# A two-layer image transformer on one core: the last tile of the merge by halves, two tiles per expert choice, the first gather from a product, the late loop elsewhere

## The chip, the cores and the metric

The kernel runs on one core of one Trainium2 chip. The metric is the device time of one execution in microseconds (us): the median of three runs before the change is 2968.36 us (2964.67 to 2971.39). Three engines matter most here. TensorE (PE; its weight loads are shown as PEld) multiplies matrices and takes its instructions strictly in their order; VectorE (DVE) and ScalarE (ACT) do the element work; GpSimd (POOL) issues the indirect transfers (gathers and scatters by a list of rows), and SyncE (SP) issues the weight loads.

## The reference, cut to what matters

Two layers (DEPTH = 2), each a mixer (retention, windowed and global attention) followed by a mixture of experts. Layer 0 has 6 tiles of 128 tokens (512 image and 256 context tokens), layer 1 only the 4 image tiles. What the change touches is the end of the mixer and the experts:

```python
y, yc = mixer_sublayer(...)            # ends with: y @ w_out
x = x + gt1 * y
h = rms_norm(x, g_norm2[l]) * (1.0 + sc2) + sh2
scores = jax.nn.sigmoid(tokens @ w_router)          # 16 experts in 4 groups
biased = scores + b_router
group_score = lax.top_k(biased by group, 2)[0].sum(-1)
group = jnp.argmax(group_score); local = lax.top_k(in_group, 2)[1]
weight = scores of the two / their sum
hid = jax.nn.silu(xb @ w_gate[e]) * (xb @ w_up[e]);  y = hid @ w_down[e]
out = for each token the weighted sum of its two experts' y
```

Everything is float32; the matrix products of the experts have D = 1024 and a hidden width of 512.

## The kernel before, in words

**Merge.** For each tile of 128 tokens `out_phase` (L1471) multiplies by `w_out` in two halves of 512 columns; `evac_o` (L1462) scales each half (`ot`) and adds it to the tile (`xo`). The generator `second(m)` (L1437) then makes the second norm (`u`, the sum of squares, `rstd`, `h`), stores `h` to `h2d`, transposes it (`h2t`, copied to `h2T`), multiplies by the router weights (`lg`) and goes on into `Router.tile` (L1985), which ranks the experts of one tile on VectorE (`rw`), counts earlier tokens by two small products (`rk`), and has GpSimd scatter a record for each token and choice (`tabd<-recs,ridx`). The table `HOOKS` says at which (half, chunk) of a later tile's product a step of `second` runs; behind the last tile a list of steps runs what is left, with nothing of the product beside it. `R.finish` (L2045) then has ACT read the records of the first three experts back (`rec<-tabd`).

**Experts.** `moe(l)` (L1538) walks 16 slots, each an expert with 12 weight chunks of 512 KB (4 of gate G, up U, down D each), so 192 loads in a layer, issued by SP in the order of use into pools of limited room (class `Weights`). The kinds of the slots are `BBBBPBSBBPBSBPBS` in layer 0 and `BBBSBSSBSSBSSBSS` in layer 1. `B` is a block of 128 tokens, whose weights are split into two words first (`wh` by ACT at L102, `wl` by DVE at L114) and whose product has three terms. `S` (class `Half`) is a block of 64 tokens that is multiplied by the unsplit weights (`raw`). `P` is a pair of both with the same weights: each chunk goes first to the block, then to the half. Each block begins with a gather of its tokens by POOL (L1549, `xg`), a transpose (`xbt`, for a half `xst`) and its evacuation by ACT (`xH`, L182).

**The late loop.** At the start of `moe` (L1771) stands `tc.For_i(0, nmore)`, a loop on all engines over blocks that did not fit their slot. `nmore` is read from memory; with these inputs it is 0, and no instruction of its body runs.

Of the kernel before, what the change touches and what calls it, by code (L numbers as in the profile page):

```python
# [16 lines left out]
D = 1024  # L17
# [9 lines left out]
LB = 2  # L27
# [10 lines left out]
class Weights:  # L38
# [95 lines left out]
    def free_raw(self, c):  # L134
        self.live[id(c.raw_pool)] -= 1
        c.raw_pool = None
        self.load()

# [9 lines left out]
def tile_dit(ctx, tc, a, out):  # L148
# [1181 lines left out]
    def merge(l):  # L1330
# [92 lines left out]
        R = Router(tc, nc, rt, small, l, nm, tri, ones, br, oac_tile, tabd[l])  # L1423
# [12 lines left out]

        def second(m):  # L1437
# [10 lines left out]
            if m == nm - 1:  # L1448
                ws.limit = last_out[l] + NEXT[l]
                ws.load()  # L1450
# [9 lines left out]
            yield from R.tile(m, lo)  # L1460

        def evac_o(m, n, ps):  # L1462
            j = 1 if m >= NIMG else 0
            c = slice(n * 512, (n + 1) * 512)
            t = page("ot1")
            nc.vector.tensor_tensor(t[:, 0:512], ps, gt1[j][:, c], op=OP.mult)
            nc.vector.tensor_tensor(xo[m][:, c], xo[m][:, c], t[:, 0:512], op=OP.add)
            if n == 1:
                load_x(m + 2)

        def out_phase():  # L1471
# [13 lines left out]
            def step(m):  # L1485

                if 0 <= m < nm:
                    if m not in steps:
                        steps[m] = second(m)
                    next(steps[m], None)  # L1490

            chunks = []
            for m in ms:
# [6 lines left out]
                if m == NIMG - 1 and nm > NIMG:  # L1500
                    at[1, 6] = lambda: mod_rows(1)
# [3 lines left out]
                for n in range(2):  # L1505
                    ps = acc_tile(f"pso_{m}{n}")
                    for k in range(8):
# [10 lines left out]
                        if k % 2:  # L1518
                            ws.pump(1)
                            if m == nm - 1:  # L1520
                                ws.free(c)
                    evac_o(m, n, ps)
            ws.set_pools(2 * l, [(raw_p, "raw", RAWB)], [],
                         [(raw_p, "raw", RAWB), (ex, "ex", EX[l]), (pool0, "pg", PG0)], [])
            last = nm - 1
            for b in (0, 1, 0, 1, 0, 2, 0, 1, 0, 0):
                step(last - b)
            for m in ms:
                assert next(steps[m], 0) == 0, m
            R.finish()  # L1530

        drive(branch_gen(), lambda: 2500)
        out_phase()
        st.close()
        return R, late, ex


    def moe(l, R, late, ex):  # L1538
# [5 lines left out]
        ws.set_pools(2 * l + 1, [(raw_p, "raw", RAWB), (pool0, "pg", PG0 - 5 * (l == 0)), (ex, "ex", EX[l])], [(mw, "mw", MW)],  # L1544
# [27 lines left out]
        class Block:  # L1572


            def __init__(self, r, pair=False, slot=None):
                self.r, self.pair, self.slot = r, pair, slot

            def fetch(self, t=None):
                self.t = mx.tile([128, D], F32, tag="xg", name="xg", bufs=XG[l]) if t is None else t
                gather(self.r, self.t)  # L1580
# [50 lines left out]
        class Half(Block):  # L1631
# [4 lines left out]
            def fetch(self):  # L1636
                self.t = mx.tile([128, D], F32, tag="xg", name="xg", bufs=XG[l])
                gather(self.r, self.t, 64)
# [100 lines left out]
        for s in range(NE):  # L1739
            kind = LINES[l][s]  # L1740
            if s < AHEAD:
                blocks.append([Block(R.rec[:, s, :])])
                continue
# [7 lines left out]
        queue = [b for bs in blocks for b in bs]  # L1751
# [19 lines left out]
        with tc.For_i(0, nc.values_load(R.nmore[0:1, 0:1], min_val=0, max_val=SLOTS)) as j:  # L1771
            late_block(j)
# [8 lines left out]
        ahead()  # L1781
        next_record()

        def gate(s, c0, c1, ps, done=None):

            for c in range(c0, c1):
                ch = ws.get()
                for i, b in enumerate(blocks[s]):
                    b.up(ps[i], *words(b, ch), c)
                    if c == 3 and done:  # L1790
                        done(i)
                used(ch)
# [11 lines left out]
        for s in range(NE):  # L1804
# [17 lines left out]
            for k in range(4):  # L1822
                ch = ws.get()
                for b in blocks[s]:
                    b.down(*words(b, ch), k)
                used(ch)
# [3 lines left out]
            for b in blocks[s]:  # L1830
                b.finish()
            if l == 0 and s == NE - 2:
# [45 lines left out]
MORE = 6  # L1878
YO = {0: 2, 1: 1}
# [13 lines left out]
HOOKS = {(0, 0): 1, (0, 1): 2, (0, 4): 1, (0, 5): 3, (1, 0): 2, (1, 3): 1}  # L1893
# [24 lines left out]
class Router:  # L1918
# [3 lines left out]
    def __init__(self, tc, nc, rt, small, l, nt, tri, ones, br, oac_tile, tabd):  # L1922
# [3 lines left out]
        self.rec = small([128, AHEAD, 4], I32, "rec")  # L1926
        self.order = small([128, NS], I32, "order")
# [10 lines left out]
    def prepare(self):  # L1938
# [28 lines left out]
        self.cumf = rt.tile([128, 7, NE], F32, name=f"cumf{l}")  # L1967
        nc.vector.memset(self.cumf[:, 0, :], 0.0)
        nc.vector.memset(self.cum[:, 0, :], 0.0)
        self.idx = rt.tile([128, 6, 2], I32, name=f"ridx{l}")  # L1970
# [14 lines left out]
    def tile(self, m, lo):  # L1985
# [3 lines left out]
        w = rt.tile([128, 16, NE], F32, tag="rw", name=f"rw{l}_{m}", bufs=2)  # L1989
        s = w[:, 0, :]  # L1990
        nc.scalar.activation(s, lo[:, 0:NE], AF.Sigmoid)
        yield
        b = w[:, 1, :]
        tt(b, s, self.br, op=OP.add)
        b4 = b.rearrange("p (g e) -> p g e", e=4)
        t0 = w[:, 2:6, :].rearrange("p a (b c) -> p a b c", b=4)
        t1 = w[:, 6:10, :].rearrange("p a (b c) -> p a b c", b=4)
        rk = w[:, 10, :].rearrange("p (g e) -> p g e", e=4)
        self.ranks(rk, b4, 4, 4, (t0, t1))
        top = w[:, 11, :].rearrange("p (g e) -> p g e", e=4)  # L2000
        stt(top, rk, 2.0, b4, op0=OP.is_lt, op1=OP.mult)
        gs = w[:, 12, 0:4]
        nc.vector.reduce_sum(gs, top, axis=AX.X)
        gr = w[:, 12, 4:8]
        self.ranks(gr[:, None, :], gs[:, None, :], 1, 4, (t0[:, 0:1], t1[:, 0:1]))
        sel = w[:, 12, 8:12]
        nc.vector.tensor_scalar(sel, gr, 0.0, None, op0=OP.is_equal)
        sel16 = sel[:, :, None].to_broadcast([128, 4, 4])
        M = w[:, 13:15, :]
        for j in range(2):  # L2010
            stt(M[:, j, :].rearrange("p (g e) -> p g e", e=4), rk, float(j), sel16, op0=OP.is_equal, op1=OP.mult)
        bb = rt.tile([128, NE], BF16, tag="bb", name=f"bb{l}_{m}", bufs=2)
        tt(bb, M[:, 0, :], M[:, 1, :], op=OP.add)
        tt(self.cumf[:, m + 1, :], self.cumf[:, m, :], bb, op=OP.add)
        nc.vector.tensor_copy(self.cum[:, m + 1, :], self.cumf[:, m + 1, :])

        two = [128, 2, NE]
        tt(w[:, 2:4, :], M, s[:, None, :].to_broadcast(two), op=OP.mult)
        ww = w[:, 15, 0:4]
        nc.vector.reduce_sum(ww[:, 0:2], w[:, 2:4, :], axis=AX.X)  # L2020
        tt(ww[:, 2:3], ww[:, 0:1], ww[:, 1:2], op=OP.add)
        nc.vector.reciprocal(ww[:, 3:4], ww[:, 2:3])
        wd = self.recs[:, m, :, 2:3].bitcast(F32)
        nc.vector.tensor_scalar(wd[:, :, 0], ww[:, 0:2], ww[:, 3:4], None, op0=OP.mult)
# [3 lines left out]
        nc.tensor.matmul(ps[:, 0:NE], self.tri, bb, start=True, stop=False)  # L2028
        nc.tensor.matmul(ps[:, 0:NE], self.ones, self.cum[:, m, :], start=False, stop=True)
        row = w[:, 4, :]  # L2030
        stt(row, ps[:, 0:NE], float(NE), self.eidx, op0=OP.mult, op1=OP.add)
        tt(w[:, 6:8, :], M, row[:, None, :].to_broadcast(two), op=OP.mult)
        nc.vector.reduce_sum(w[:, 15, 4:6], w[:, 6:8, :], axis=AX.X)
        nc.vector.tensor_copy(self.idx[:, m, :], w[:, 15, 4:6])
        for j in range(2):
            nc.gpsimd.memset(self.spacer, 0.0)
            st = nc.gpsimd.indirect_dma_start(
                out=self.tabd, out_offset=bass.IndirectOffsetOnAxis(ap=self.idx[:, m, j:j + 1], axis=0),
                in_=self.recs[:, m, j, :], in_offset=None)
            for o in self.scat:  # L2040
                self.tc.declare_no_dep(st.ins, o.ins, reason="each record has a row of its own")
            self.scat.append(st)
# [194 lines left out]
```

## Time and profile before

| | |
|---|---|
| runs (us) | 2971.39, 2968.36, 2964.67 (median 2968.36) |
| the profiled execution (us) | 2971.79, of which its span 2970.0 |
| mean granted TensorE clock | 0.969 |
| busy: PE, DVE, ACT, POOL | 2774.9 (93%), 1835.0 (62%), 1279.9 (43%), 355.3 (12%) |
| moved by DMA | 557.63 MB, 188 GB/s over the span |
| PE's share of the chain that ended last | 27% by named lines, DMA 6%, DVE 3% |

The span is the time from the first to the last instruction, so what lies around it is 1.8 us. Busy shares are means over stages with different limits: the two expert stages (about 1345 to 1650 us and 2683 to 2946 us of the span) move more than 340 GB/s, the stages before them far less. In the rows a column "[x <-E y]" behind an instruction says how long its engine was idle before it and what ended that.

### The profile page before, as it was taken

The numbers are of one execution on the slowest core, as the hardware profiler recorded it, in microseconds if no ns is written. First come the engines' busy times: TensorE is split into PE (matmuls) and PEld (weight loads), VectorE is DVE, ScalarE is ACT, GpSimd is POOL, SyncE is SP. The second block draws the span as 40 slices with busy tenths as digits, with TensorE's granted clock in tenths as the row PEclk, the third lists the DMA queues.
The fourth block names the chain that finished last, engine by engine and source line by source line (L and its number), as shares of the span: only waits on it lengthen the run. The fifth ranks groups of instructions, "written<-read, shape, count | busy, mean of one in ns | idle before, by whom it ended". The sixth has DMA issues, their size and how long they took to land. (4 is left out here: it accounts for less than half of the span.)

```text
span 2970.0 us, 41952 instructions
## 1 busy us (share of the span) xinstructions
PE 2774.9 (93%) x15152; PEld 2221.7 (75%) x15152; DVE 1835.0 (62%) x3340; ACT 1279.9 (43%) x2370; POOL 355.3 (12%) x415
## 2 busy tenths in 40 slices
PE   7999999999999999979999699999999999978985
PEld 4888888888888766767666378878888887767653
DVE  4676567666554455677676566667776655677543
ACT  4444445445443211217575354444455442226332
POOL 1220000000010000022222131100000100012311
PEclk8999999999999999989999899999999999988998
DMA  6333222213243566758999732222223447589997
GB/s 240 131 110 105 89 75 91 91 65 103 100 156 118 211 240 238 273 225 304 328 370 363 256 122 82 89 78 97 75 96 123 146 153 285 207 304 341 370 367 293
DMA packets 201910, 557.63 MB, mean 188 GB/s; under 512 B 25158, under 2 KB 49862, under 8 KB 201696
## 3 DMA queue, kind: packets, MB, share of 16 engines
q1 hardware_dynamic: 173888, 503.63, 47.0%
q0 software_dynamic: 10688, 25.02, 3.5%
q10 hardware_dynamic: 17120, 26.23, 2.4%
q8 instruction: 121, 1.98, 0.3%
q14 instruction: 93, 0.76, 0.1%
HBM read 461.94 MB, written 96.77 MB: 188 GB/s over the span
## 5 line engine op out<-in xcount | busy, mean ns | idle before, releaser
L114 DVE TENSOR_TENSOR wl<-raw,wh 128x1024 fp32r<-128x1024 f32 x474 | 564.6, 1221 | 130.7 <-ACT wh L102 123.8
L102 ACT CAST wh<-raw 128x1024 fp32r<-128x1024 f32 x474 | 484.4, 1050 | 352.0 <-DMA raw<-oT 105.0
L887 ACT ACTIVATE P<-sc,st 128x768 f32<-128x768 f32 (+4 forms) x240 | 176.3, 734 | 339.9 <-DVE st L885 213.4
L885 DVE TENSOR_REDUCE st<-sc 128x1 f32<-128x768 f32 (+4 forms) x240 | 178.6, 744 | 121.5 <-PE sc L174 115.7
L174 PE MATMUL psb<-wl,wh 128*128 128x512 f32 x480 | 189.6, 395 | 8.1 <-DVE wl L114 8.0
L921 ACT CAST ptH<-pt 128x512 fp32r<-128x512 f32 x264 | 142.9, 591 | 125.0 <-PE pt L906 104.5
L174 PE MATMUL psb<-wh,wh 128*128 128x512 f32 x480 | 192.9, 402 | 1.7 <-ACT wh L102 1.7
L174 PE MATMUL psb<-wh,wl 128*128 128x512 f32 x480 | 189.1, 394 | 2.0 <-DVE wl L114 2.0
L931 DVE TENSOR_TENSOR ptL<-pt,ptH 128x512 fp32r<-128x512 f32 x264 | 169.6, 681 | 9.3 <-ACT ptH L921 9.1
L906 PE MATMUL pt<-ident,P 128*128 128x128 f32 x1056 | 141.5, 275 | 13.9 <-ACT P L887 10.9
L906 PEld LDWEIGHTS pt<-ident,P 128*128 128x128 f32 x1056 | 119.5, 141 | 45.2 <-ACT P L887 31.3
L174 PE MATMUL psR<-wh,hH 128*128 128x512 f32 (+1 forms) x384 | 150.8, 393 | 0.0
L174 PE MATMUL psR<-wl,hH 128*128 128x512 f32 (+1 forms) x384 | 147.1, 383 | 2.7 <-DVE wl L114 2.7
L174 PE MATMUL psR<-wh,hL 128*128 128x512 f32 (+1 forms) x384 | 147.6, 384 | 0.0
L893 DVE TENSOR_SCALAR P<-P,st 128x768 f32<-128x768 f32 (+3 forms) x240 | 130.0, 542 | 8.5
L174 PEld LDWEIGHTS psb<-wh,wh 128*128 128x128 f32 x480 | 91.1, 190 | 47.5 <-issue 19.3
L481 POOL TENSOR_SCALAR rstd<-ss 128x4 f32<-128x4 f32 (+2 forms) x70 | 22.0, 314 | 835.3 <-ACT h L487 303.1
L174 PEld LDWEIGHTS psb<-wl,wh 128*128 128x128 f32 x480 | 91.1, 190 | 29.1 <-DVE wl L114 11.5
L174 PE MATMUL sc<-swkT,swqs 128*128 128x256 f32 x704 | 109.1, 281 | 2.2 <-ACT P L887 2.2
L174 PEld LDWEIGHTS psb<-wh,wl 128*128 128x128 f32 x480 | 91.1, 190 | 22.9 <-DVE wl L114 3.6
L174 PE MATMUL yps<-wh,hidT 128*128 128x512 f32 x320 | 105.7, 397 | 0.0
L1094 DVE COPY sc<-sink 128x1 f32<-128x1 f32 x160 | 25.7, 161 | 128.5 <-PE sc L174 122.3
(495 smaller groups left out, 6916.4 us busy)
## 6 DMA issues: line engine op xcount, KB each, us to landing
raw<-in_w_in_dram SPq DMA_DIRECT2D x136, 512.0 KB
raw<-in_w_gate_dram SPq DMA_DIRECT2D x128, 512.0 KB
raw<-in_w_up_dram SPq DMA_DIRECT2D x128, 512.0 KB
raw<-in_w_down_dram SPq DMA_DIRECT2D x128, 512.0 KB
raw<-in_w_mod_dram SPq DMA_DIRECT2D x96, 512.0 KB
raw<-in_w_br_dram SPq DMA_DIRECT2D x48, 512.0 KB
raw<-oT SPq DMA_DIRECT2D x30, 512.0 KB
raw<-in_w_out_dram SPq DMA_DIRECT2D x16, 512.0 KB
```

The source lines that it names most:

```text
L102: self.nc.scalar.copy(c.h, c.raw)
L114: self.nc.vector.tensor_tensor(c.l, c.raw, c.h.bitcast(F32), op=OP.subtract)
L174: nc.tensor.matmul(ps, lhs, rhs, start=start, stop=stop, skip_group_check=share)
L481: nc.gpsimd.tensor_scalar(r[:, 0:cnt], ss, four / n, four * EPS, op0=OP.mult, op1=OP.add)
L885: nc.vector.reduce_max(st[:, 1, h:h + 1], s[:, 0:self.ns], axis=AX.X, negate=True)
L887: nc.scalar.activation(self.P[h][:, 0:self.ns], s[:, 0:self.ns], AF.Exp, bias=st[:, 1, h:h + 1], accum_out=st[:, 2, h:h + 1])
L893: nc.vector.tensor_scalar(self.P[h][:, 0:self.nk], self.P[h][:, 0:self.nk], st[:, 3, h:h + 1], None, op0=OP.mult)
L906: nc.tensor.transpose(pt[:, c * 256 + h * 128:c * 256 + (h + 1) * 128], self.P[2 * x + h][:, i * 128:(i + 1) * 128], ident)
L921: nc.scalar.copy(ph, src)
L931: nc.vector.tensor_tensor(pl, src, ph.bitcast(F32), op=OP.subtract)
L1094: nc.vector.tensor_copy(s[:, nk:nk + 1], sink[:, hd:hd + 1])
```

## The change

1. The last tile of the merge is worked by halves (class `Last`): squares and `u` of a half as soon as that half is added, its transposes and half of its scores inside the second half's product, and the norm factor applied to the scores (`scores = r * (u @ w_router) + sh2 @ w_router`) rather than to the tokens first; the shift's row is made by nine small products (`shift`).
2. `Router.pair` in place of `Router.tile`: ranks of two tiles in one set of instructions; `HOOKS` gets other places.
3. For the first three experts the row list `first` is made by products of 0/1 matrices (`oh`) with the row numbers (`idc`), and POOL gathers the first block (`x0`) by it before the last pair's scatters. The first three blocks gather by `first`.
4. The late loop stands behind slot 10 in layer 0 and slot 13 in layer 1.
5. In a `P` slot the half's products run behind the block's four chunks (`chunk`), no longer between them.
6. One buffer fewer for late blocks (`LB`), and one page fewer for the weights of layer 1 (x0 holds it).

```diff
-LB = 2
+LB = 1
...
+            def stat(self, n):
+                nc.scalar.activation(self.h[:, c], xo[last][:, c], AF.Square, accum_out=self.ss[:, n:n + 1])
+                nc.vector.tensor_tensor(self.u[:, c], xo[last][:, c], g2[j][:, c], op=OP.mult)
...
+            def end(self):
+                self.norm()
+                self.turn(1)
+                nc.vector.scalar_tensor_tensor(self.h, self.u, self.r[:, 0:1], sh2[j], op0=OP.mult, op1=OP.add)
+                nc.sync.dma_start(h2d[l][last * 128:(last + 1) * 128, :], self.h)
+                nc.sync.dma_start(xa[l][last], xo[last])
+                ws.limit = last_out[l] + NEXT[l]
+                ws.load()
+                self.score(1)
+                s = sg_of(last)
+                nc.vector.scalar_tensor_tensor(s, self.lo[:, 0:NE], self.r[:, 0:1], self.shw, op0=OP.mult, op1=OP.add)
+                nc.scalar.activation(s, s, AF.Sigmoid)
...
+                if m == last:
+                    at[0, 3] = L.begin
+                    at[0, 6] = L.shift
+                    at[1, 6] = lambda: L.turn(0)
...
-            for b in (0, 1, 0, 1, 0, 2, 0, 1, 0, 0):
-                step(last - b)
+            L.end()
+            step(last - 1)
...
+            x0 = pool0.tile([128, D], F32, tag="pg", name=f"x0{l}")
+            for _ in R.pair(last - 1, sg[last // 2], x0):
+                pass
             R.finish()
...
-        with tc.For_i(0, nc.values_load(R.nmore[0:1, 0:1], min_val=0, max_val=SLOTS)) as j:
-            late_block(j)
         ws.limit = first_in + NEAR if l == 0 else len(ws.specs)
         ws.load()
...
+        def chunk(bs, c, step, done=None):
+            ch = ws.get()
+            step(0, c, words(bs[0], ch))
+            if c == 3 and done:
+                done(0)
+            if len(bs) == 1:
+                used(ch)
+                return
+            ws.pump(2, LEAD)
+            ws.free_parts(ch)
+            kept.append(ch)
+            if c == 3:
+                for i, ch in enumerate(kept):
+                    step(1, i, words(bs[1], ch))
+                    ws.free(ch)
...
             for b in blocks[s]:
                 b.finish()
+            if s == LOOPAT[l]:
+                with tc.For_i(0, nc.values_load(R.nmore[0:1, 0:1], min_val=0, max_val=SLOTS)) as j:
+                    late_block(j)
...
+LOOPAT = {0: 10, 1: 13}
-HOOKS = {(0, 0): 1, (0, 1): 2, (0, 4): 1, (0, 5): 3, (1, 0): 2, (1, 3): 1}
+HOOKS = {(0, 0): 1, (0, 4): 1, (0, 5): 2, (1, 1): 1, (1, 5): 1, (1, 7): 1}
...
+    def pair(self, m, s, x0=None):
+        for e in range(AHEAD):
+            oh = rt.tile(shape, BF16, tag="oh", name=f"oh{l}_{m}{e}", bufs=2)
+            tt(oh, self.places[:, None, :].to_broadcast(shape), f[:, :, e:e + 1].to_broadcast(shape), op=OP.is_equal)
+            for i in range(4):
+                nc.tensor.matmul(psf[:, e:e + 1], oh[:, i // 2, :], self.idc[:, i % 2, m + i // 2:m + i // 2 + 1],
+                                 start=i == 0, stop=i == 3)
+            if x0 is not None:
+                tt(self.first[:, e:e + 1], self.firstf[:, e:e + 1], psf[:, e:e + 1], op=OP.add)
+                if e == 0:
+                    nc.gpsimd.indirect_dma_start(
+                        out=x0, out_offset=None, in_=self.h2d,
+                        in_offset=bass.IndirectOffsetOnAxis(ap=self.first[:, 0:1], axis=0))
```

POOL, end of layer 1's merge, before: the last scatters of the records, then the first gather (`xg<-h2d`, by the records that were read back), then the loop.

```order
L2036 MEMSET spacer 1x1
L2037 DMA tabd_122<-recs_23670,ridx_23693 14336x4
L1549 DMA xg<-h2d_119,rec 128x1024
L1771 TENSOR_LOAD nmore
L1771 COMPARE_AND_BRANCH
```

The same place now: L2173 is the gather of `x0` by `first`, L2204 a scatter, L1650 the gather of the second block.

```order
L1531 TENSOR_TENSOR ss<-ss 128x1
L486 TENSOR_SCALAR rstd<-ss 128x1
L487 TENSOR_TENSOR rstd<-rstd,nhalf 128x1
L2173 DMA x_24942<-h2d_119,first 128x1024
L2203 MEMSET spacer 1x1
L2204 DMA tabd_122<-recs_23677,ridx_23705 14336x4
```

The first gather moved ahead of the last pair's four scatters, and the loop left this place.

SP, layer 1, before: the loop's exit (L1771; its body stands ahead of it) is followed by the loads of most of the layer (L83).

```order
L1771 COMPARE_AND_BRANCH
L1771 UNCONDITIONAL_BRANCH
L83 DMA raw_25236<-in_w_up_dram 128x1024
L83 DMA raw_25238<-in_w_up_dram 128x1024
L83 DMA raw_25240<-in_w_up_dram 128x1024
L83 DMA raw_25242<-in_w_up_dram 128x1024
L1776 TENSOR_LOAD order
```

Now the loop (L1949) stands behind the layer's last load; here with the waits printed (`DMAHW0` to `DMAHW7` are the counters of the weight loads):

```order
L83 DMA raw_26987<-in_w_down_dram 128x1024 [waits DMAHW1_49]
L83 ISA
L83 DMA raw_26995<-in_w_down_dram 128x1024 [waits DMAHW2_49,DVE_49]
L1949 TENSOR_LOAD nmore
L1949 ISA x2
L1949 COMPARE_AND_BRANCH
L1949 UNCONDITIONAL_BRANCH [waits SP_sequencer_49,DMAHW0_49,DMAHW1_49,DMAHW2_49,DMAHW3_49,DMAHW4_49,DMAHW5_49,DMAHW6_49,DMAHW7_49]
```

On SP no weight load of layer 1 is left behind the loop, and its exit waits for all eight counters of the loads.

PE, layer 1, the first product of slot 14 (a half; U, then G) before, with the waits:

```order
L1643 MATMUL xst<-ident,xg 128x64 x7
L174 MATMUL u<-raw_27016,xs 64x256 [waits DMAHW1_49]
L174 MATMUL u<-raw_27016,xs 64x256 x3
L174 MATMUL u<-raw_27027,xs 64x256 [waits DMAHW2_49]
L174 MATMUL u<-raw_27027,xs 64x256 x3
```

The same products now, directly behind the loop:

```order
L1745 MATMUL xst<-ident,xg 128x64 x8
L179 MATMUL u<-raw_26834,xs 64x256 x4
L179 MATMUL u<-raw_26840,xs 64x256 x4
L179 MATMUL u<-raw_26847,xs 64x256 x4
L179 MATMUL u<-raw_26851,xs 64x256 x4
L179 MATMUL g<-raw_26855,xs 64x256 [waits Activation_49]
```

The products of the last two slots no longer wait for a load, each of which had its own wait before.

## Rows read from the trace of the kernel before

**Rows 1.** Busy time by stretch: us; PE, PEld, DVE, ACT, POOL; clock; DMA share; GB/s.

```profile
1220.00:1310.00 90.00, 90.00 (x487) 75.11 (x485) 65.77 (x162) 23.72 (x36) 10.36 (x22) 1.00 0.66 248
1310.00:1340.00 30.00, 6.23 (x33) 5.76 (x33) 17.40 (x80) 3.52 (x7) 9.04 (x16) 0.55 0.71 272
1340.00:1350.00 10.00, 7.07 (x19) 5.18 (x20) 5.16 (x5) 6.18 (x6) 3.38 (x3) 0.50 0.34 106
...
1400.00:1650.00 250.00, 250.00 (x1308) 172.14 (x1308) 164.07 (x159) 156.41 (x179) 58.95 (x39) 1.00 0.98 349
2590.00:2650.00 60.00, 60.00 (x312) 49.69 (x311) 43.42 (x92) 16.12 (x23) 4.42 (x10) 1.00 0.82 302
2650.00:2680.00 30.00, 7.51 (x45) 7.03 (x44) 18.49 (x80) 4.03 (x8) 8.12 (x15) 0.57 0.69 255
2680.00:2690.00 10.00, 8.80 (x26) 6.55 (x27) 6.05 (x6) 6.72 (x7) 3.38 (x3) 0.57 0.80 271
...
2700.00:2800.00 100.00, 98.32 (x562) 69.80 (x562) 65.78 (x67) 51.14 (x62) 25.41 (x18) 1.00 1.03 372
...
2918.00:2946.00 28.00, 22.42 (x143) 9.17 (x141) 3.90 (x7) 1.71 (x4) 3.14 (x2) 1.00 0.86 317
```

**Rows 2.** The chain that ended last, end of layer 1: start, us, what.

```profile
2934.19 10.49 DMA raw<-in_w_down_dram
```

**Rows 3.** Timeline of PE, the last two slots of layer 1.

```profile
2918.50 0.71 PE L1643 MATMUL xst<-ident,xg 64*128 64x64 f32 x8
...
2941.85 3.96 PE L174 MATMUL ysm<-raw,hidS 128*64 128x512 f32 x16 [0.52 <-ACT hidS L1674]
```

**Rows 4.** Timeline of VectorE, both merges' ends: start, us, engine line op.

```profile
1308.57 0.69 DVE L1466 TENSOR_TENSOR ot<-pso,m 128x512 f32<-128x512 f32 x1 [0.23 <-PE pso L174]
...
2649.84 0.69 DVE L1466 TENSOR_TENSOR ot<-pso,m 128x512 f32<-128x512 f32 x1 [0.24 <-PE pso L174]
...
2654.86 0.23 DVE L1979 TENSOR_TENSOR rw<-rw 128x64 f32<-128x64 f32 x1
...
2667.57 0.34 DVE L2084 TENSOR_TENSOR sq<-bw 128x169 f32<-128x169 f32 x1
```

**Rows 5.** Timeline of PE in layer 0's experts.

```profile
1344.86 0.79 PE L174 MATMUL g<-wh,xH 128*128 128x512 f32 x1 [1.10 <-ACT xH L182]
...
1546.44 0.39 PE L174 MATMUL yps<-wh,hidT 128*128 128x512 f32 x1
...
1556.71 0.71 PE L1643 MATMUL xst<-ident,xg 64*128 64x64 f32 x8
...
1567.35 0.50 PE L174 MATMUL yps<-wh,hidT 128*128 128x512 f32 x1
...
1572.93 1.03 PE L493 MATMUL xbt<-ident,xg 128*128 128x128 f32 x8
...
1583.41 3.65 PE L174 MATMUL ysm<-raw,hidS 128*64 128x512 f32 x16
```

**Rows 6.** The chain that ended last, end of layer 1's merge.

```profile
2660.44 15.71 DMA tabd<-recs,ridx
2676.15 3.91 issue
...
2683.12 1.22 PE g L174 x2
```

**Rows 7.** Timeline of POOL, then of ACT, end of layer 1's merge.

```profile
2669.04 0.96 POOL L2037 DMA_INDIRECT tabd<-recs,ridx  x1 [0.21 <-issue]
2673.99 0.99 POOL L1549 DMA_INDIRECT xg<-h2d,rec  x1 [3.99 <-SPq L1771]
...
2671.16 0.33 ACTq L2050 DMA_DIRECT2D rec<-tabd  x1
```

**Rows 8.** The loop's line on SP: count, shortest/median/longest ns, first and last start.

```profile
L1771 SPq EVENT_SEMAPHORE  x42: 17/28/28, 1330.0 to 2679.1; - x42
```

**Rows 9.** What SP waited for from 2668 to 2682: us in total, times, longest.

```profile
SPq L1771 <- DMA xg<-h2d,rec: 2.8, 1, 2.8
```

More of the change, by code (lines that the diff above doesn't have):

```diff
@@ L1435, in load_x, with sg_of @@
                 nc.sync.dma_start(xo[m], x_src(m))
+        last = nm - 1
+        sg = {}
+        def sg_of(m):
+            if m // 2 not in sg:
+                sg[m // 2] = rt.tile([128, 2, NE], F32, tag="sg", name=f"sg{l}_{m}", bufs=2)
+            return sg[m // 2][:, m % 2, :]
         def second(m):
@@ L1459, in second, with begin, shift, load_col @@
                 mm(lo[:, 0:NE], hf[:, k * 128:(k + 1) * 128], wr[:, k, :], k == 0, k == 7)
-            yield from R.tile(m, lo)
+            nc.scalar.activation(sg_of(m), lo[:, 0:NE], AF.Sigmoid)
+            yield
+            if m % 2:
+                yield from R.pair(m - 1, sg[m // 2])
+        class Last:
+            def begin(self):
+                self.h = page(f"h2_{l}_{last}")
+                self.u = page(f"u_{l}_{last}")
+                self.hf = page(f"h2T{l}_{last}")
+                self.ss = small([128, 8], F32, "ss", bufs=4)
+            def shift(self):
+                j = 1 if last >= NIMG else 0
+                ps = oac_tile("shr")
+                for k in range(8):
+                    mm(ps[0:1, 0:NE], self.col[:, k:k + 1], wr[:, k, :], k == 0, k == 7)
+                row = rt.tile([1, NE], F32, name=f"shrow{l}")
+                nc.scalar.copy(row, ps[0:1, 0:NE])
+                ps2 = oac_tile("shb")
+                mm(ps2[:, 0:NE], self.one, row, True, True)
+                self.shw = rt.tile([128, NE], F32, name=f"shw{l}")
+                nc.scalar.copy(self.shw, ps2[:, 0:NE])
+            def load_col(self):
+                j = 1 if last >= NIMG else 0
+                self.col = rt.tile([128, 8], F32, name=f"shcol{l}")
+                self.one = rt.tile([1, 128], F32, name=f"onerow{l}")
+                nc.gpsimd.memset(self.one, 1.0)
+                nc.sync.dma_start(self.col, modd[l][j, 3, :].rearrange("(k p) -> p k", p=128))
+            def stat(self, n):
+                j = 1 if last >= NIMG else 0
+                c = slice(n * 512, (n + 1) * 512)
+                nc.scalar.activation(self.h[:, c], xo[last][:, c], AF.Square, accum_out=self.ss[:, n:n + 1])
+                nc.vector.tensor_tensor(self.u[:, c], xo[last][:, c], g2[j][:, c], op=OP.mult)
+            def turn(self, n):
+                ps = oac_tile(f"u2t{l}_{n}")
+                for k in range(4):
+                    c = slice((4 * n + k) * 128, (4 * n + k + 1) * 128)
+                    nc.tensor.transpose(ps[:, k * 128:(k + 1) * 128], self.u[:, c], ident)
+                o = n * 512
+                if n == 0:
+                    nc.scalar.copy(self.hf[:, 0:512], ps)
+                else:
+                    nc.scalar.copy(self.hf[:, o:o + 256], ps[:, 0:256])
+                    nc.vector.tensor_copy(self.hf[:, o + 256:o + 512], ps[:, 256:512])
+            def score(self, n):
+                if n == 0:
+                    self.lo = oac_tile(f"lg{l}_{last}")
+                for k in range(4 * n, 4 * n + 4):
+                    mm(self.lo[:, 0:NE], self.hf[:, k * 128:(k + 1) * 128], wr[:, k, :], k == 0, k == 7)
+            def norm(self):
+                nc.gpsimd.tensor_tensor(self.ss[:, 2:3], self.ss[:, 0:1], self.ss[:, 1:2], op=OP.add)
+                self.r = rstd_of(self.ss[:, 2:3], D, 1)
+            def end(self):
+                j = 1 if last >= NIMG else 0
+                self.norm()
[9 more added lines that the diff above has]
+                nc.scalar.activation(s, s, AF.Sigmoid)
@@ L1750, in moe @@
             blocks.append(bs)
-        queue = [b for bs in blocks for b in bs]
+        queue = [b for bs in blocks[1:] for b in bs]
+        blocks[0][0].t = x0
         later = [b for b in queue if b in records]
@@ L1926, in __init__ @@
         self.rec = small([128, AHEAD, 4], I32, "rec")
+        self.first = small([128, AHEAD], I32, "first")
         self.order = small([128, NS], I32, "order")
@@ L1999, in tile, with by_group @@
[L1999 to L2002, printed above, removed]
+        w = rt.tile([128, 22, 2, NE], F32, tag="rw", name=f"rw{l}_{m}")
+        def by_group(t):
+            return t.rearrange("p j (g e) -> p (j g) e", e=4)
+        b = w[:, 0]
+        tt(b, s, self.br[:, None, :].to_broadcast([128, 2, NE]), op=OP.add)
+        t0, t1 = (w[:, i:i + 4].rearrange("p a j (g e) -> p (a j g e)", e=4).rearrange("p (g a c) -> p g a c", g=8, a=4)
+                  for i in (1, 5))
@@ L2007, in tile @@
+        sel = w[:, 11, 1, 0:8]
         nc.vector.tensor_scalar(sel, gr, 0.0, None, op0=OP.is_equal)
[L2008 to L2024, printed above, removed]
+        sel4 = sel[:, :, None].to_broadcast([128, 8, 4])
@@ L2030, in tile @@
[L2030 to L2034, printed above, removed]
-        for j in range(2):
[L2036 to L2042, printed above, removed]
+        for j in range(2):
+            o = ps[:, j * NE:(j + 1) * NE]
+            nc.tensor.matmul(o, self.tri, bb[:, j, :], start=True, stop=False)
+            nc.tensor.matmul(o, self.ones, self.cum[:, m, :], start=False, stop=j == 0)
+            if j:
+                nc.tensor.matmul(o, self.ones, bb[:, 0, :], start=False, stop=True)
@@ new lines, in pair @@
+        nc.vector.reciprocal(sm, sm)
+        tt(self.recs[:, m:m + 2, :, 2].bitcast(F32).rearrange("p j k -> p k j"), ww,
+           sm[:, None, :].to_broadcast([128, 2, 2]), op=OP.mult)
+        for j in range(2):
+            for k in range(2):
+                nc.gpsimd.memset(self.spacer, 0.0)
+                st = nc.gpsimd.indirect_dma_start(
+                    out=self.tabd, out_offset=bass.IndirectOffsetOnAxis(ap=self.idx[:, m + j, k:k + 1], axis=0),
+                    in_=self.recs[:, m + j, k, :], in_offset=None)
+                for o in self.scat:
+                    self.tc.declare_no_dep(st.ins, o.ins, reason="each record has a row of its own")
+                self.scat.append(st)
```

132 lines of the change are left out of this document (84 added, 48 removed).

## The prediction

> **What bounds the kernel now.** I read the page first, then the busy time by stretch, the chain of waits, and the timelines at the ends of the stages. The stretches show four regimes [rows 1]. In the last 90 and 60 us of the merges PE is busy without a gap. Then come some 30 us per layer (1310 to 1340, 2650 to 2680) in which it works 6.23 and 7.51 us: the last tile's norm, its expert choice, the records and the first gather, one after the other. In layer 0's experts PE is busy 250 of 250 us and the DMA engines are at 0.98, so both are nearly full. In layer 1's experts the DMA share is 1.03 at 372 GB/s: the weight loads bound that stage, and its last load lands at 2934.19 + 10.49 = 2944.68 [rows 2], 1.1 us before PE's last product ends at 2941.85 + 3.96 = 2945.81 [rows 3]. So four things must be priced: the two gaps, what is put into the gapless merges, layer 0's experts, and what stands between the last load and the end.
>
> **The gaps.** From the last `ot` to the first expert product: 1308.57 to 1344.86 in layer 0, 2649.84 to 2683.12 in layer 1 [rows 4, 5, 6], so 36.3 and 33.3 us. On the chain the records' scatters and their landing take 15.71 us and the next 3.91 us name no work [rows 6]. In them lie the last scatter (2669.04), ACT's read of the records (2671.16), the gather (2673.99) [rows 7], and the loop, which SP leaves at 2679.1 [rows 8].
> The changed tail by the same rows: both halves of the last add 1.4 us, norm and scores about 5 (a norm, four transposes, four score products instead of eight of each), some 17 ranking steps of 0.25 at a row's 0.23 for 64 columns [rows 4] about 4, the products for `first` about 2: the gather is issued near 12, and, with the 5.1 us that lay between its issue at 2673.99 and the loop's last event at 2679.1 [rows 7, 8], lands near 18. But the records' read stands on ACT ahead of the evacuation `xH`. Four scatters at the pitch of 1.3 from 14.5 end near 19, the read is issued 2.1 us behind the last one (2671.16 against 2669.04 [rows 7]), then transpose and `xH`: first product at about 25.7. Low end 21 (ACT waits for nothing), high end no gain. I take 25.7, since the read kept its place: **-10.6 and -7.5 us**.
>
> **What goes into the merges.** PE takes its instructions in order. In a pair's second part it waits for VectorE three times (a 0/1 matrix of 256 columns, estimated at 0.34 x 256/169 = 0.5 us from [rows 4]) and once for the row it is built from: about 2.5 us, and `w_out`'s products queue behind. Two pairs lie inside layer 0's product, one inside layer 1's; the shift's row adds about 2 in each (product, copy by ACT, product). As PE has no idle time there [rows 1], this is paid: **+7 and +4.5 us**. Bounds: 0, if VectorE is always ahead; 12 and 8, if its queue holds other work of 1 to 2 us each time.
>
> **The P slots.** D of slot 9, alternating, takes 1546.44 to 1556.71, 10.27 us; the same sixteen steps apart, D of slot 10's block, 1567.35 to 1572.93, and a half's D, 3.65, take 5.58 + 3.65 = 9.2 [rows 5]. Layer 0 has three P slots of three such products: 9 x 1.04 = **-9 us**, PE being full there; at the least -5, as the loads are nearly full too.
>
> **The loop.** Its body never runs, and still each pass costs SP 21 semaphore events (42 in two) [rows 8], and it sat 2.8 us of that on the first gather [rows 9]. So the way past the loop waits for every transfer issued so far. The order says the same: SP's exit names all eight load counters, and the products behind it have lost their waits for loads. At the start of `moe` little was in flight but that gather; at the new places the load stream is.
> *Layer 1, behind slot 13.* No load is left behind the loop on SP, so PE stands until the last one has landed, and then has all of slots 14 and 15 to do. Before, that work filled 22.42 of the 28 us from 2918 to 2946 [rows 1], while the last loads came in. Now it starts behind them. After the two gaps the clock was 0.50 and 0.57 for some 10 us [rows 1]: at half clock for 8 us, 4 us more. So the stage ends about 0.7 + 22.4 + 4 = 27 us after the last load, where it ended 1.1 after: +26. Against it, the loads start with the earlier tail (-7.5 + 4.5 = -3), and the load of `gf` (one 512 KB transfer, 1.4 us at 372 GB/s) no longer lies among them. As the fall of the DMA share before the end is gradual, the last weights may land up to 3 us before the chain's 2944.68, which takes up to 3 off. I take **+20 us** for the layer's end, all of this and the -7.5 and +4.5 included; bounds +13 (clock stays up) and +26.
> *Layer 0, behind slot 10.* SP has loads left, so only those in flight must land. The last load of the trace took 10.49 us from its issue [rows 2], and the same depth gives PE 10 to 13 idle us with the half clock's 4 behind: **+16**. Bounds: +8, if half of them have landed by the time, and +22, if the stream, which stands too, then starves PE again.
> The Trainium skill, page "DMA: Bandwidth & Descriptors", section "Rules for kernel authors", speaks against such a place: issue a transfer early, compute, and wait on its semaphore late. Were the waits as late as before, layer 1 would come out at -3 and not +20; the loop's rows show that they are early [rows 8, 9]. The same page ("Specifications") gives about 358 GB/s as one core's share of the memory; by it the 15 loads that are left at 2918 would take 22 us instead of the 21 that 372 GB/s give, and the sum would rise by 1.
>
> **Sum.** Layer 0: -10.6 + 7 - 9 + 16 = +3.4. Layer 1: +20. Together +23 on the profiled execution's 2971.8 us gives 2995; the median of the runs lies 3.4 below that execution, so **2991 us**. About 0.2%, 6 us, is what a measurement can tell from no change: 2962.4 to 2974.3 is "same".
>
> **Rivals.**
> A. *The way past the loop carries no waits when the count is 0* (faster). Place: the exit of L1949; price: the two drains of 16 and 23 us vanish. Then -10.6 + 7 - 9 in layer 0 and -3 in layer 1: -16, 2952 us. It decides if PE goes on with slot 14 while loads are still landing. For it: the old loop's 8 us can mostly be put down to a gather that was needed anyway. Against it: 21 events a pass and the wait on the gather [rows 8, 9], and that those products have no wait of their own left. 0.11.
> B. *The drains are there but small* (same): layer 0's costs 6, since SP runs ahead and PE reaches the loop with little in flight, PE waits for nothing in the merges (-7 and -4), and the clock stays up (-4). Then 2991 - 10 - 11 - 4 = 2966, or up to 2970 if the clock falls. For it: VectorE is busy less than three quarters of the merges [rows 1]. Against it: three things must go well at once. 0.13.
> C. *The drain of layer 0 starves what follows* (slower still). PE is full and the DMA share is 0.98 there [rows 1], so the stream has no slack to make up the 10 us in which it stands; with waits of 12 and 8 us in the merges: +6 and +9, 3006 us. 0.18.
> D. *The early gather buys nothing*: the records' read holds ACT until after the old time, so the gaps stay. +18, 3009 us. Against it: scatters end 1.3 us apart and the norm is earlier anyway. 0.03.
> The forecast has 0.55.
>
> **Range and chances.** Case A's 0.11 and about half of D and C's upper part are left out. From below it takes in B, from above the bounds of the loop and of the merges: 2964 to 3008. Faster 0.12 (A and a little of B), same 0.11 (B), slower 0.77 (the forecast, C, D).
>
> **What would show it.** The loop's line in layer 1: PE idle some 20 us before slot 14, no weight load after it, then 22 to 26 us of PE with the DMA share near 0. In layer 0 a gap of 10 us or more behind slot 10 with the clock near 0.5 behind it. The gaps at the merges' ends 25 to 26 us long, the gather issued before the last scatters. The P slots' D near 9.2 us. PE short of full by some 7 us in layer 0's last 90 merge us. The forecast is wrong if PE crosses the loop while loads land, or if the time is under 2964.

## The result and the profile after

The changed kernel took 3015.92 us in the median of four runs (3013.33 to 3018.8) against 2967.76 for the kernel before; the ratio is 1.0162, 95% interval 1.0144 to 1.018. It is slower, as forecast, but by 48 us and not 23, and outside the range (2964 to 3008). The profiled execution took 3013.33 us with a span of 3011.5, 41.5 more than before. That is less than the 48 us between the medians, because the profiled execution of the kernel before (2971.79) lay above its runs and that of the changed kernel is the fastest of its four; the stages below, with what lies around them, add up to the 41.5.

Busy time by stretch of the changed kernel (columns as in [rows 1]): the merge of layer 0, three short stretches inside it, the gap behind it, the stretch behind slot 10, the merge of layer 1, its gap, and the two stretches at the end of layer 1.

```profile
1224.00:1326.00 102.00, 93.51 (x516) 77.23 (x514) 55.64 (x116) 22.52 (x39) 12.53 (x27) 0.93 0.61 226
1305.00:1310.00 5.00, 1.59 (x12) 1.07 (x10) 3.99 (x6) 1.15 (x2) 0.78 (x3) 1.00 1.04 350
1310.00:1315.00 5.00, 4.17 (x35) 3.02 (x36) 2.92 (x15) 0.33 (x2) 1.15 (x2) 0.61 0.97 372
1315.00:1320.00 5.00, 5.00 (x21) 4.01 (x21) 2.07 (x3) 1.43 (x4) 3.06 (x6) 0.71 1.03 381
...
1326.00:1351.00 25.00, 6.03 (x48) 4.73 (x46) 15.48 (x59) 3.44 (x7) 7.89 (x14) 0.61 0.61 232
1576.00:1587.00 11.00, 0.00 (x1) 0.00 (x0) 0.00 (x0) 1.11 (x1) 1.62 (x1) 0.72 0.74 259
2607.00:2674.00 67.00, 62.76 (x344) 51.83 (x343) 36.84 (x68) 16.01 (x27) 6.66 (x15) 0.92 0.72 272
2674.00:2700.00 26.00, 6.82 (x42) 5.21 (x41) 15.59 (x58) 4.20 (x8) 8.49 (x14) 0.55 0.68 246
...
2938.00:2965.00 27.00, 1.05 (x6) 0.57 (x5) 1.50 (x2) 0.00 (x0) 1.56 (x1) 0.59 0.79 298
2965.00:2988.00 23.00, 21.50 (x140) 10.94 (x139) 2.68 (x5) 1.72 (x4) 1.56 (x1) 0.89 0.12 30
```

Against [rows 1]: the merges are no longer full (93.51 of 102 us, 62.76 of 67) and their clock is below 1 (a figure between 0.50 and 1.00 is a stretch that holds both half and full clock); each gap is shorter; and there are two new holes, 11 us behind slot 10 and 27 us ahead of slot 14, where the weights of the last two slots land (298 GB/s) while PE is busy for 1.05 us. Then PE works 21.5 of 23 us with the DMA engines nearly idle.

TensorE's timeline in the changed kernel, at the two waits in layer 0's merge, in the gap behind it, behind slot 10, and at the end of layer 1:

```profile
1275.03 0.60 PE L2168 MATMUL first<-idc,oh 128*128 128x1 bf16 x8 [4.00 <-DVE oh L2166]
...
1306.42 0.17 PE L2157 MATMUL rk<-bb,ones 128*128 128x16 bf16 x1
1310.26 0.59 PE L2168 MATMUL first<-idc,oh 128*128 128x1 bf16 x8 [3.68 <-DVE oh L2166]
...
1345.50 1.97 PE L498 MATMUL xbt<-ident,x 128*128 128x128 f32 x8 [6.58 <-DMA x<-h2d,first]
1350.88 0.79 PE L179 MATMUL g<-wh,xH 128*128 128x512 f32 x1 [3.41 <-ACT xH L187]
...
1587.56 1.97 PE L498 MATMUL xbt<-ident,xg 128*128 128x128 f32 x8 [11.55 <-issue]
...
2938.45 0.40 PE L179 MATMUL yps<-wh,hidT 128*128 128x512 f32 x1
2964.80 1.11 PE L1745 MATMUL xst<-ident,xg 64*128 64x64 f32 x8 [25.95 <-SPq L1949]
...
2983.96 3.65 PE L179 MATMUL ysm<-raw,hidS 128*64 128x512 f32 x16 [0.52 <-ACT hidS L1776]
```

VectorE at the second of the merge's waits:

```profile
1306.25 1.23 DVE L1457 TENSOR_TENSOR u<-xo,m 128x1024 f32<-128x1024 f32 x1
1308.39 1.28 DVE L1460 SCALAR_TENSOR_TENSOR h<-u,rstd,m 128x1024 f32<-128x1024 f32 x1 [0.91 <-POOL spacer L2203]
1309.59 0.16 DVE L2161 SCALAR_TENSOR_TENSOR rw<-rk,bb 128x6 f32<-128x6 f32 x1
1309.78 1.20 DVE L2166 TENSOR_TENSOR oh<-places,rw 128x256 bf16<-128x256 bf16 x3
```

The counting products end at 1306.6. VectorE has what it needs from them then, but first makes `u` and `h` of the next tile, between them 0.91 us idle until POOL has the norm's factor; the row for the 0/1 matrices (`rw`) comes at 1309.59 and the matrices (`oh`) from 1309.78 on. PE stands at the first product that needs them, and `w_out`'s products stand behind that.

By stage, from the starts of TensorE's products in the two profiles, the last one of a stage counted to the end of its step (merge: first to last product with `w_out`; gap: from there to the first expert product; experts: from there to the last expert product):

| stage | before | after | difference | forecast |
|---|---|---|---|---|
| merge, layer 0 | 82.8 | 101.1 | +18.4 | +7 |
| gap, layer 0 | 36.5 | 24.9 | -11.6 | -10.6 |
| experts, layer 0 | 318.7 | 326.8 | +8.1 | +7 (-9 + 16) |
| mixer and branches, layer 1 | 933.2 | 930.4 | -2.8 | 0 |
| merge, layer 1 | 52.9 | 65.1 | +12.2 | +4.5 |
| gap, layer 1 | 33.5 | 25.9 | -7.6 | -7.5 |
| experts, layer 1 | 263.0 | 288.8 | +25.8 | +23 |

The forecast's sum falls 18 us short of the profiled difference: the two merges lie 19 us over it, and the other stages nearly cancel.

### The profile page after: what moved, and what is told of

Read it like the earlier page. It is cut to its first block, busy times and chain, and to the rows that moved or that the text cites. A ratio compares the mean times of both kernels' runs of the same rounds, so it can differ in the third digit from the quotient of the medians.

```text
span 3011.5 us, 42058 instructions
## 1 busy us (share of the span) xinstructions
PE 2788.7 (93%) x15253; PEld 2235.7 (74%) x15253; DVE 1822.4 (61%) x3235; ACT 1279.0 (42%) x2376; POOL 363.3 (12%) x425
## 5 line engine op out<-in xcount | busy, mean ns | idle before, releaser
L1099 DVE COPY sc<-sink 128x1 f32<-128x1 f32 x160 | 25.8, 161 | 128.7 <-PE sc L179 122.5
```

Of the source, the lines that this page charges most:

```text
L1099: nc.vector.tensor_copy(s[:, nk:nk + 1], sink[:, hd:hd + 1])
```

## Experiments

The theory to test had three parts: the loop's drains are what was forecast; the merges' waits and the half clock behind them make the rest; and a smaller effect, found in the two traces, is that the three-term products of the experts step every 233 ns (227 before). The rival for the first two was that the loads start later or find less room, so that layer 1 ends late whatever the loop does.

**The loop back at the start, all else as changed.** `LOOPAT = {0: -1, 1: -1}`, with

```diff
+        if LOOPAT[l] < 0:
+            with tc.For_i(0, nc.values_load(R.nmore[0:1, 0:1], min_val=0, max_val=SLOTS)) as j:
+                late_block(j)
         ws.limit = first_in + NEAR if l == 0 else len(ws.specs)
```

> The changed kernel with the late loop back at the start of the experts in both layers, all else as changed. Theory (the loop at slots 10 and 13 waits for the loads in flight): layer 0 loses the idle 11.6 us behind slot 10 and some 2 us of half clock, layer 1 ends about 1 us after its last load instead of 22; the loop at the start costs some 4 us a layer before the first product. 3016 - 14 - 21 + 8 = 2989 us. Rival (layer 1 ends late because its loads start later or find less room, whatever the loop does): only layer 0's part comes back, 3016 - 14 + 8 = 3010 us.

Measured: 2991.51 us, ratio to before 1.0079 (1.0062 to 1.0095). TensorE's timeline, the gap of layer 0 and the last product:

```profile
1362.29 1.97 PE L498 MATMUL xbt<-ident,x 128*128 128x128 f32 x8 [20.02 <-issue]
1365.36 0.79 PE L179 MATMUL g<-wh,xH 128*128 128x512 f32 x1 [1.10 <-issue]
...
2965.29 1.08 PE L179 MATMUL ysm<-raw,hidS 128*64 128x512 f32 x4 [0.17 <-DMA raw<-in_w_down_dram]
```

The rival falls: layer 1's experts take 262.7 us again, with the last product behind the last load. Layer 0's take 307.7, so the loop at slot 10 cost 19 us and the grouped products save 11. Some 3.5 of the 19 are not the loop's waits but the longer step of the products, which this kernel does not have (227 ns; see the pitch below). The gaps are 36.8 and 34.2 us, as long as before: with the loop there, the early gather and the split last tile shorten neither.

**The loop alone, on the kernel before**: the same three lines taken from L1771 and put behind `b.finish()` with `LOOPAT = {0: 10, 1: 13}`.

> The kernel before with nothing changed but the late loop's place: behind slot 10 in layer 0, slot 13 in layer 1. Theory: +12 us idle and some 2 us of half clock in layer 0, +21 us at the end of layer 1, less some 4 us at each layer's start, where the first gather is no longer waited for with the loop: 2968 + 14 + 21 - 6 = 2997 us. Rival (the drain is small and the losses come from the merges and the loads): 2968 to 2980 us.

Measured: 3004.72 us, ratio 1.0127 (1.011 to 1.0144). Its two holes in TensorE's timeline:

```profile
1580.41 1.97 PE L493 MATMUL xbt<-ident,xg 128*128 128x128 f32 x8 [11.01 <-issue]
...
2951.16 1.11 PE L1643 MATMUL xst<-ident,xg 64*128 64x64 f32 x8 [26.03 <-SPq L1831]
```

In the changed kernel they are 11.55 and 25.95 us; here nothing else of the change is there. The loop alone costs 36 us, and the gaps it leaves are 33.2 and 35.1 us: moving it gives the gap little unless the tail is changed too. The estimate was 8 us low: it took 6 us off for the gaps, which gave back 3.3 and lost 1.6, and it gave layer 0's experts 14 us, where they take 17.4 longer (their products step every 233 ns here too).

**Where the loop is cheap.** `LOOPAT = {0: -1, 1: 15}` and `{0: 15, 1: 15}` in the changed kernel.

> The changed kernel with the late loop at the start of the experts in layer 0 and behind the last slot (15) in layer 1. Theory: the loop costs what is in flight and still to do behind it; behind slot 15 all loads have landed and no product is left, so layer 1 keeps its short end (about 26 us from the merge's last product to the first expert product, 34 with the loop there) and ends 1 to 3 us behind its last load: 2991.5 - 8 + 2 = 2985 us. Rival (a loop anywhere late in layer 1 costs its 20 us, for instance since it delays the loads): above 3000 us.

> The changed kernel with the late loop behind slot 15 in both layers. Theory: in layer 0 the loads of the next layer are in flight there, so TensorE stands some 10 us and runs at half clock after it, against 12 us that the short end of the merge gives and some 5 us for the slower pitch of 233 ns: 2985 - 12 + 5 + 13 = 2991 us. Rival (nothing that matters is in flight at the layer's end): 2978 us.

Measured: 2987.38 us (ratio 1.0073, 1.0057 to 1.0088) and 2991.79 us (1.0083, 1.0067 to 1.0098). With the loop behind slot 15 of layer 1, the last product and the stretches about it (columns as in [rows 1]) are these:

```profile
2953.12 4.02 PE L179 MATMUL ysm<-raw,hidS 128*64 128x512 f32 x16 [0.52 <-ACT hidS L1776]
...
2950.00:2953.00 3.00, 1.85 (x14) 0.69 (x10) 0.42 (x1) 0.30 (x1) 0.13 (x1) 1.00 0.66 193
2953.00:2957.00 4.00, 3.73 (x16) 0.97 (x16) 0.00 (x0) 0.07 (x1) 0.00 (x0) 1.00 0.08 22
```

The loads run out about 2953 and the last product ends at 2957.1, some 4 us behind them. Layer 1's experts take 266.8 us there (263.0 before), what follows the last product takes 3 us more, and the gap stays at 25.9. So it is in the main not a late loop as such that costs: it is the loads in flight and the work still to come. In layer 0 the end is no better a place than the start: the gap is 10 us shorter, but the experts take 6.6 us and the next layer's mixer 7 us longer.

**The pair's second part cut in two.** The counting products and the 0/1 matrices run at (0,1), the products with them at (0,7):

```diff
+        if x0 is None:
+            for e in range(AHEAD):
+                one_hot(e)
+            yield
-HOOKS = {(0, 0): 1, (0, 4): 1, (0, 5): 2, (1, 1): 1, (1, 5): 1, (1, 7): 1}
+HOOKS = {(0, 0): 1, (0, 1): 2, (0, 4): 1, (0, 7): 2, (1, 1): 1, (1, 5): 1, (1, 7): 1}
```

> The changed kernel with the pair's second part cut in two: counting products and 0/1 matrices at (0,1), ahead of the next tile's norm on VectorE, and the products with the 0/1 matrices six chunks later at (0,7). Theory (inside the merges TensorE stands 4 us for each pair, since the 0/1 matrices queue behind the next tile's norm, and runs at half clock after it): two such places in layer 0, one in layer 1; -12 and -7 us: 2997 us, and the gaps of 4 us are gone from TensorE's timeline. Rival (VectorE has too much to do in the merge, so the wait comes back at the next evacuation): above 3010 us.

Measured: 2998.7 us, ratio 1.0095 (1.0078 to 1.0113). The merges take 91.0 and 58.4 us instead of 101.1 and 65.1. TensorE between the two parts:

```profile
1299.08 0.17 PE L2154 MATMUL rk<-bb,tri 128*128 128x16 bf16 x1 [1.00 <-DVE bb L2145]
...
1304.81 0.46 PE L2180 MATMUL first<-idc,oh 128*128 128x1 bf16 x12
```

The clock where the changed kernel had 0.61 and 0.71 behind its wait (columns as in [rows 1]):

```profile
1300.00:1305.00 5.00, 4.66 (x41) 3.45 (x40) 4.15 (x7) 1.49 (x4) 0.84 (x3) 1.00 1.00 342
1305.00:1310.00 5.00, 5.00 (x37) 4.24 (x34) 3.95 (x15) 1.05 (x3) 1.96 (x3) 1.00 1.00 371
```

The twelve products no longer wait. Two waits of 4.0 and 3.7 us in layer 0 and one of 3.9 in layer 1 are gone, but not all of it is gained: the counting products now wait 1.0 us each time, and in layer 0 another product waits 1.1, so the waits fall by 4.9 and 2.8 us. The merges gain 10.1 and 6.7; the rest goes with the full clock that TensorE now keeps: the products with `w_out` alone take 4.0 and 2.4 us less.

**Both cures together**: this split and `LOOPAT = {0: -1, 1: 15}`.

> The changed kernel with both cures: the pair's second part cut in two as in the run with the split, and the late loop at the start in layer 0 and behind slot 15 in layer 1. Theory (the merges' waits and the loop's drains are separate costs and add): 2987.4 - 10.1 - 6.7 = 2971 us. Rival (what the merges lose is given back elsewhere, for instance since the loads start earlier): above 2980 us.

Measured: 2970.01 us, ratio 1.001 (1.000 to 1.002). The costs add, and without them the change comes out even. By its profile the merges still take 7.0 and 5.5 us more than before (89.8 and 58.4 us), and the loop behind slot 15 costs 3.6 us in layer 1's experts and 3.2 behind them; the grouped products in layer 0 (9.7 us) and layer 1's shorter gap (7.4) pay for that.

**The first gather late.** The gather of `x0` moved behind the last pair's scatters.

```diff
                 self.scat.append(st)
+        if x0 is not None:
+            nc.gpsimd.indirect_dma_start(
+                out=x0, out_offset=None, in_=self.h2d,
+                in_offset=bass.IndirectOffsetOnAxis(ap=self.first[:, 0:1], axis=0))
         yield
```

> The changed kernel with the first gather (x0) issued behind the last pair's four scatters, not ahead of them, still by the rows from the 0/1 products. Theory (the gather's way is the longer one as soon as it is not early): issued 9 us later, landing 8.5 us behind that, while ACT is free at about the old time; the first expert product comes 6 to 7 us later in each layer, of which layer 1 may hide a part behind its loads: 3023 to 3029 us. Rival (ACT's read of the records holds the evacuation of the first block anyway, so the early gather buys nothing): 3016 us.

Measured: 3020.08 us, ratio 1.0179 (1.0162 to 1.0196). POOL issues it at 1343.75 and TensorE has it at 1348.26:

```profile
1343.75 0.99 POOL L2207 DMA_INDIRECT x<-h2d,first  x1 [0.30 <-issue]
```

```profile
1348.26 1.97 PE L498 MATMUL xbt<-ident,x 128*128 128x128 f32 x8 [11.65 <-DMA x<-h2d,first]
1351.45 0.80 PE L179 MATMUL g<-wh,xH 128*128 128x512 f32 x1 [1.22 <-ACT xH L187]
```

The gaps are 28.7 and 28.1 us, 3.8 and 2.2 longer than with the early gather. Neither theory had it right. The early gather, issued at 1337.01 with scatters behind it, took 8.5 us to be used, the late one 4.5 (9.5 and 4.4 in layer 1). ACT's read of the records in the changed kernel, and with the late gather:

```profile
1348.22 0.33 ACTq L2217 DMA_DIRECT2D rec<-tabd  x1
```

```profile
1345.11 0.33 ACTq L2217 DMA_DIRECT2D rec<-tabd  x1
```

Counted from the last product of layer 0's merge the read comes at 22.2 and at 22.3 us, so the early gather leaves it where it was. In the changed kernel ACT was held by this read until 1348.9 and then by one weight chunk, and the first product waited 3.41 us for `xH`: there the read sets the gap's end, and with the late gather the gather does.

**The pitch of the experts' products.** Three kernels: the tile of the first rows 32 words wide instead of 3 (all later buffers 96 bytes further), and an unused tile of 64 bytes (as printed) or of 192 (48 words) at the head of the pool `mx`:

```diff
-        self.first = small([128, AHEAD], I32, "first")
+        self.first = small([128, 32], I32, "first")[:, 0:AHEAD]
```

```diff
+        spare = mx.tile([128, 16], F32, tag="spare", name="spare", bufs=1)
+        nc.vector.memset(spare, 0.0)
```

> The changed kernel with the tile of the first three experts' rows made 32 words wide instead of 3, which moves every later buffer by 96 bytes, back to addresses that are multiples of 64 (the 3-word tile had moved them by 32). Theory (the three-term products of the experts step every 233 ns instead of 227 because of the addresses of their operands): 227 ns again, some 24 x 3 x 13 products in layer 0 at 6 ns, -5.6 us, and 0 to -3 us in layer 1, whose loads bound it: 3008 to 3011 us. Rival (the pitch comes from the other order of the products or from the loop): 233 ns and 3016 us.

> The changed kernel with an unused tile of 64 bytes at the head of the pool that holds the experts' tokens and hidden words (xH, xL, hidT), which moves these from 96 to 32 bytes past a multiple of 128; loop and order as changed. Theory (a three-term product steps every 227 ns with those operands less than 64 bytes past a multiple of 128, as in the kernel before and with the loop at the start, and every 233 ns otherwise): 227 ns in both layers, -5.6 us in layer 0, 0 to -3 in layer 1: 3007 to 3011 us. Rival (the pitch follows the loop's place or the order of the code, not the address): 233 ns, 3016 us.

> The changed kernel with an unused tile of 192 bytes at the head of the pool of the experts' tokens and hidden words, which puts xH, xL and hidT at the same place within 512 bytes (and within 8192) as in the kernel with the loop at the start, which stepped every 227 ns. Theory (the pitch depends on an address within 512 or more bytes): 227 ns, 3008 to 3011 us. Rival (it follows the loop's place, not the addresses): 233 ns, 3013 to 3016 us.

Measured: 3009.17 us (ratio 1.0142, 1.0125 to 1.0159), 3015.88 (1.0162, 1.0149 to 1.0176) and 3013.32 (1.0161, 1.0138 to 1.0183). The median step of layer 0's D products is 233, 232 and 227 ns. The 24 D products of slot 0, first product and the transpose that follows them, in the changed kernel (one more row of it), with 64 and with 192 bytes:

```profile
1371.54 0.39 PE L179 MATMUL yps<-wh,hidT 128*128 128x512 f32 x1
...
1377.14 1.03 PE L498 MATMUL xbt<-ident,xg 128*128 128x128 f32 x8
```

```profile
1370.41 0.39 PE L179 MATMUL yps<-wh,hidT 128*128 128x512 f32 x1
...
1375.99 1.04 PE L498 MATMUL xbt<-ident,xg 128*128 128x128 f32 x8
```

```profile
1368.08 0.39 PE L179 MATMUL yps<-wh,hidT 128*128 128x512 f32 x1
...
1373.52 1.03 PE L498 MATMUL xbt<-ident,xg 128*128 128x128 f32 x8
```

5.60, 5.58 and 5.44 us. Two guesses at the address (a multiple of 64, within 128 bytes) fell; the third held: with the loop late and the buffers where they lie with the loop early, the step is 227 ns. The loop's body allocates three small tiles in that pool, and moving it moves every buffer behind them; `xH` then starts 480 bytes past a multiple of 512, against 128 before. Which addresses are slow is not settled beyond that: 448 (the loop alone), 64 and 32 past are slow too, 160 is fast. The kernel with the loop early in layer 0 alone agrees: 160 past and 227 ns there, 480 past and 235 ns in layer 1. Its worth is small: layer 0's experts take 323.3 us instead of 326.8, the run's time lies in its rival's range and not in the theory's, and it differs from the changed kernel's by less than its interval. The first of the three came out at 3009.17, inside its theory's range, with the step still 233 ns: that is luck. Its profile is 5.7 us shorter in layer 1's experts, and no run here shows why.

**The grouped products alone, on the kernel before**: `chunk` and `free_parts`, and nothing else.

> The kernel before with the pairs' half products run behind the block's four chunks, and nothing else of the change. Theory: nine products in layer 0 at 1.0 to 1.2 us less each, TensorE being full there: 2968 - 10 = 2958 us, the experts' stage of layer 0 308 us instead of 319. Rival (the loads are as near to their limit there): 2964 us or more, with waits for loads in layer 0.

Measured: 2957.67 us (2951.89 to 2958.74), ratio 0.9968 (0.9956 to 0.998): faster than both kernels. The experts of layer 0 take 307.7 us, the merges and gaps are as before. A pair's D, from its first product to the transpose behind it:

```profile
1443.40 0.39 PE L179 MATMUL yps<-wh,hidT 128*128 128x512 f32 x1
...
1448.94 3.65 PE L179 MATMUL ysm<-raw,hidS 128*64 128x512 f32 x16
1452.52 0.71 PE L1648 MATMUL xst<-ident,xg 64*128 64x64 f32 x8
```

The half's 16 products take 3.6 us in a row; alternating, the same slot's D took 10.3 us for both, now 9.1.

## Why the prediction was right and wrong

**The loop** was right in both layers and in its mechanism: the way past a loop that never runs waits for what is in flight. Layer 1 has a wait of 25.95 us ahead of slot 14 and 23 us of work behind the loop; the forecast's price for the stage was +23, measured +25.8 (+21.8 with the loop alone on the kernel before). Of the half clock the forecast had 4 us; PE worked at 0.89 over the last stretch. Layer 0 measured +19 for +16. Some 3.5 of that is the longer step that came with the moved buffers, which the forecast did not have; with the step at 227 ns the loop there costs 15.6 us (323.3 less 307.7). Rival A (no waits on the way past) fell with the first hole in the trace, and the loop alone on the kernel before shows it without the rest.

**The gaps** measured -11.6 and -7.6 for -10.6 and -7.5, and the reason given held: ACT's read of the records came after the gather had landed, and `xH` behind it. The gather took 8.5 us from issue to use, where the forecast had about 6 to its landing; the read hid that. Rival D fell, since the gaps did get shorter, but little of it is the early gather's (3.8 and 2.2 us).

**The P slots** measured -11 for -9; no wait of TensorE for a load shows in layer 0's experts.

**The step that failed is "What goes into the merges"**: +18.4 and +12.2 for +7 and +4.5, outside its own bounds of 12 and 8. Its terms against the two traces, in us, layer 0 and layer 1 (the time from one product's start to the next's, waits apart):

| term | forecast | measured |
|---|---|---|
| waits for the 0/1 matrices | 5 and 2.5 | 8.0 and 3.9 |
| the shift's row, its wait included | 2 and 2 | 1.4 and 1.4 |
| `w_out`'s products, slower at half clock | 0 and 0 | 5.1 and 3.2 |
| other work moved in, and the rest | 0 and 0 | 3.9 and 3.8 |

Two terms were put at nothing. One is the clock behind a wait, which was counted for the loop but not here: it stood at 0.61 and 0.71 in the two 5 us windows behind the second wait. The other is work that the change moves into the merges from the gaps: the score products of one more tile (16 on TensorE, 1.7 us), four transposes of the last tile and the products for `first`. And each wait was sized by the row and the three 0/1 matrices, 2.5 us, as if VectorE came to them at once; it was 3.7 to 4.0, because `u` and `h` of the next tile stand ahead on that engine. The forecast's sign for the merge, PE short of full by some 7 us, came out at 8.5 us: the idle time alone does not show the miss. The run with the pair cut in two shows the waits and the clock by taking them away. That the rest is the work moved in is read from the traces; no run takes it out.

**Rival C** came nearest in time (3006) and had waits of 12 and 8 us in the merges, but its own cause did not show: behind the hole in layer 0 the loads did not starve TensorE, which was busy 12.44 of the 13 us from 1587 to 1600. **Rival B** (small drains) fell; what it would have given, an even result, needed two edits.

By the Trainium skill, page "TensorE: Matmul & The Clock Gate", section "Part 1: The HAM clock gate", an idle TensorE goes to the lower of its two clocks. The rows agree: PE was busy 1.59 of the 5 us up to 1310, at full clock, and the clock was 0.61 in the 5 us after.

## What to carry to other kernels

Put a wait into a stage where an in-order engine is full, and its price is the queue ahead on the engine it waits for, plus the clock that it loses afterwards; read that queue in the order of the changed program before sizing the wait, and count the work that comes with it. Full clock in the trace of before is no promise for the trace of after. A loop that may run zero times is still a place where every engine and every transfer in flight meet: it belongs where little is in flight and little work is left. When several parts are changed at once, try each alone: of the two parts that were tried alone here, the grouped products gained 9 us and the loop's new places lost 36. The split last tile, the pairs, the early gather and the smaller buffers (parts 1 to 3 and 6) were not run alone, the gather's place only within the changed kernel, so what each of them costs or saves is not shown.

## What the runs showed of the hardware

Moving buffers by 192 bytes changed the step of identical 512-column products from 233 to 227 ns, some 2.6%, with the same order of the products (5.60 against 5.44 us for 24). And a gather of 128 rows took 8.5 and 9.5 us (layers 0 and 1) from issue to use with four scatters issued behind it, 4.5 and 4.4 us when it was issued behind them; whether the scatters are the cause was not tried apart.

The way past a loop whose body never ran held TensorE 11 to 12 us in layer 0 and 26 us in layer 1 while loads were in flight, in both kernels.
